# The down projection of a SwiGLU layer as one step of Strassen's scheme in four passes

## The chip, the core and the metric

The kernel runs on one core of a Trainium2 chip, in one launch. The core has five engines with an instruction stream each: TensorE (PE in the profile) multiplies matrices into PSUM, VectorE (DVE) and GpSimd (POOL) work elementwise, ScalarE (ACT) casts and evaluates functions, and SyncE (SP) issues the transfers between DRAM (HBM) and SBUF. The metric is the device time of one execution in microseconds (us), smaller is better. The median of three runs of the kernel before is 1910.74 us.

## What is computed

One layer of an encoder on 1152 rows (1024 frames of a prompt and 8 x 16 frames of running streams) of width 1024: three token mixers side by side, a cross-attention, and a SwiGLU feed-forward network, each with a residual add, and a final RMSNorm. The change touches the last matrix product of the feed-forward network, the residual add behind it, and the final norm.

```python
D_MODEL = 1024
...
D_FF = ((8 * D_MODEL + 3 * 256 - 1) // (3 * 256)) * 256   # 2816
EPS = 1e-6
...
def rmsnorm(x, g):
    xf = x.astype(jnp.float32)
    y = xf * lax.rsqrt(jnp.mean(xf * xf, axis=-1, keepdims=True) + EPS)
    return (y * g.astype(jnp.float32)).astype(x.dtype)
...
def swiglu(u, wg, wu, wd):
    hdn = jax.nn.silu(jnp.einsum('bnd,df->bnf', u, wg)) * jnp.einsum('bnd,df->bnf', u, wu)
    return jnp.einsum('bnf,fd->bnd', hdn, wd)
...
    h = h + swiglu(rmsnorm(h, p['norm_ffn_g']), p['w_gate'], p['w_up'], p['w_down']).astype(h.dtype)
...
    y_prompt = rmsnorm(hp, final_norm_g)
    y_sample = rmsnorm(hs, final_norm_g)
```

All of it is in float32.

## The kernel before

The kernel is one long program; each engine executes its instructions in the order in which a scheduler placed them, and waits for what they read. A tile from a pool with n buffers can be written again only when the readers of the tile n places earlier are done. Large products are taken in three matmuls on halves of the mantissa: each operand x is split into hi (a cast by ACT, L1697) and lo = x - hi (a subtraction by VectorE, L1701), and hi·hi + hi·lo + lo·hi is accumulated in PSUM (`mm3`, L328 to L330).

The last stages are these. Gate/up (`gate_up`, L1857 for its matmuls) makes the hidden rows of the feed-forward network, 22 tiles of 128 features by 1152 rows. It uses a scheme of seven products already: its right and left factors are sums of blocks (L1705, L1713, `sub`), split with POOL (L132) or VectorE, and its results are recombined from PSUM by VectorE (L1832). ACT and VectorE multiply the two branches (L1837, L1838), and SP stores each tile to the DRAM scratch `hid_sc` (L1839).

The down projection follows. It takes the rows in three chunks c of 384. For each of the 22 feature tiles f, SP loads a hidden tile of 128 x 384 (L1977, 192 KB) and a row block of w_down of 128 x 1024 (L1978, 512 KB); both are split; then three blocks of 128 rows times two column halves times three make 18 matmuls of 512 columns, accumulated over f in six of the eight PSUM banks:

```python
for i in range(3):
    for j in range(2):
        products(ops, i, j, f == 0, f == NFT - 1)
```

Behind each of the first two chunks `finish` adds the residual rows (loaded from `h_sc`), squares them on ACT, takes the power -1/2 on POOL with one Newton step on VectorE, scales (L1942) and stores. The last chunk holds back its last three f, and multiplies them block by block, so that `finish_by_halves` (L1952 to L1963) works on one block while PE multiplies the next. POOL has nothing but those small powers in this stage. All loads of the stage are issued by SP in order, and the stores of hidden and output rows stand in the same queue.

Of the kernel before, what the change touches and what calls it, by code (L numbers as in the profile page):

```python
# [17 lines left out]
P = 128  # L18
# [39 lines left out]
def f32(x):  # L58
    return x.bitcast(F32)
# [3 lines left out]
def tile_hybrid_step(ctx: ExitStack, tc: tile.TileContext, a: dict):  # L63
# [1599 lines left out]
    rawp = ctx.enter_context(f_pool("rawp", 2))  # L1663
    up = ctx.enter_context(f_pool("up", 3))
    tmp = ctx.enter_context(f_pool("tmp", 1))
    tlp = ctx.enter_context(f_pool("tlp", NL))
# [227 lines left out]
    trp = ctx.enter_context(f_pool("trp", NR, "right"))  # L1894
# [22 lines left out]
    bstack.close()  # L1917


    fin = ctx.enter_context(f_pool("fin", 1))  # L1920
# [5 lines left out]
    banks = [pd, pd, pS, pS, pT, pT, pT, lambda: o_all]  # L1926
    HALF = [slice(j * 512, (j + 1) * 512) for j in range(2)]

    def store_rows(b, j0, j1, y):
        cl = slice(j0 * 512, j1 * 512)  # L1930
        dst = a["y_prompt"][0, b * P:(b + 1) * P, cl] if b < 8 else a["y_sample"].rearrange("b q d -> (b q) d")[:, cl]
        SP.dma_start(out=dst, in_=y[:, cl])

    def finish(b, x, acc):

        for j in range(2):
            DVE.tensor_tensor(out=x[:, HALF[j]], in0=x[:, HALF[j]], in1=acc[j], op=ALU.add)
        y = fin.tile([P, D], F32, tag="y", name="y", bufs=4)
        ss = small(1)
        ACT.activation(y, x, AF.Square, accum_out=ss)  # L1940
        r = rstd_of(ss, 1, 1.0 / D)
        DVE.scalar_tensor_tensor(y, x, r, gF, ALU.mult, ALU.mult)  # L1942
        store_rows(b, 0, 2, y)

    def finish_by_halves(b, x):

        y = fin.tile([P, D], F32, tag="y", name="y", bufs=4)
        v, r, t, r2 = small(2), small(1), small(1), small(1)

        def half(j, acc):  # L1950
            ss = small(1)
            DVE.tensor_tensor(out=x[:, HALF[j]], in0=x[:, HALF[j]], in1=acc, op=ALU.add)  # L1952
            ACT.activation(y[:, HALF[j]], x[:, HALF[j]], AF.Square, accum_out=ss)
            if j == 0:
                DVE.tensor_scalar(v[:, 0:1], ss, 1.0 / D, EPS, ALU.mult, ALU.add)
                return
            DVE.scalar_tensor_tensor(v[:, 1:2], ss, 1.0 / D, v[:, 0:1], ALU.mult, ALU.add)
            POOL.tensor_tensor(out=r, in0=v[:, 1:2], in1=mhalf, op=ALU.pow)
# [76 lines left out]
```

## Time and profile before

| | |
|---|---|
| runs, device time | 1910.74 us median (1908.35 to 1920.12) |
| profiled execution, span from first to last instruction | 1911.2 us |
| mean granted clock of TensorE | 0.989 |
| first and last matmul of the down projection start | 1626.41 and 1902.21 us |

The page gives no time of the profiled execution outside its span. How to read the rows further on: the views list instructions, or groups of them, with their engine (PEld is the loading of TensorE's stationary operand), the line of the kernel, the operation, the tiles out<-in, partitions x elements and the count (x4). In a timeline the first number is the start and the second the duration in us, or for a group the time from the first start to the last end; in brackets stands the idle time ahead of it and what ended it. In the view by groups the busy time and the mean duration in ns of one stand behind the first bar, the idle time before and its releasers behind the second. In the view by stretches, busy time and count stand for each engine, then the granted clock, the busy share of the DMA engines and GB/s. The matmul rows' durations overlap, since matmuls are pipelined; the spacing of their starts is what one costs.

### The profile page before, as it was taken

To read this page: it belongs to the slowest core of one execution; us is meant where nothing else is said; L and a number is where in the kernel's file an instruction comes from. 1 tells how busy PE (TensorE), PEld (TensorE's weight loads), DVE (VectorE), ACT (ScalarE), POOL (GpSimd) and SP (SyncE) were. 2 spreads that over 40 slices of the span, in tenths; PEclk is the share of its full clock that TensorE was granted. 3 is DMA by queue.
4 is the path that set the end of the run, shared out by engine and by line. 5 is a ranking of instruction groups with operands and counts; after the bars stand their busy time and mean duration, and the time that the engine had idled before them with its cause. 6 is when DMAs were issued, how large, how long until landed. Compare 5 with 4: busy or idle time off the path is not lost.

```text
span 1911.2 us, 32463 instructions
## 1 busy us (share of the span) xinstructions
PE 1834.5 (96%) x12120; PEld 1637.6 (86%) x12120; DVE 894.3 (47%) x1823; ACT 822.7 (43%) x1779; POOL 627.9 (33%) x923
## 2 busy tenths in 40 slices
PE   7989988999998899999999999999999999999998
PEld 5889876888876677899998889999999999788886
DVE  3421323557656882354444487333333333455554
ACT  6531543535666870344343275333333333344443
POOL 7632416254224662211112105454444542000000
PEclk9999998999999999999999999999999999999999
DMA  9455645536579896345567124223322223566672
GB/s 338 141 165 159 207 139 129 161 102 186 174 237 291 268 323 217 111 144 162 180 210 270 61 83 119 70 71 81 88 73 70 70 70 104 188 196 228 183 245 91
DMA packets 302365, 306.07 MB, mean 160 GB/s; under 512 B 82428, under 2 KB 253668, under 8 KB 302208
## 3 DMA queue, kind: packets, MB, share of 16 engines
q1 hardware_dynamic: 302208, 304.01, 51.4%
q8 instruction: 95, 1.56, 0.3%
q14 instruction: 62, 0.51, 0.1%
HBM read 229.84 MB, written 74.63 MB: 159 GB/s over the span
## 4 chain that ended last, share of the span: by engine, by line
PE 81%; DMA 6%; DVE 3%; POOL 3%; issue 3%; ACT 2%; SPq 1%; POOLq 0%; DVEq 0%; ACTq 0%
PE psd L1857 11%; PE psd L328 10%; PE psd L329 10%; PE psd L330 9%; PE pst L1857 8%; PE pss L1857 4%; PE pss L328 3%; PE pss L329 3%; PE pss L330 3%; PE pso L1857 2%; PE pso L594 2%; PE pst L328 1%; PE pst L329 1%; PE pst L330 1%; POOL wl L132 1%
## 5 line engine op out<-in xcount | busy, mean ns | idle before, releaser
L132 POOL TENSOR_TENSOR wl<-wr,wh 128x256 fp32r<-128x256 f32 (+2 forms) x184 | 140.9, 800 | 219.4 <-ACT wh L292 215.7
L328 PE MATMUL psd<-act,wh 128*128 128x384 f32 x576 | 199.2, 346 | 4.8 <-DVE sg L455 2.7
L329 PE MATMUL psd<-act,wh 128*128 128x384 f32 x576 | 197.9, 344 | 0.0
L330 PE MATMUL psd<-act,wl 128*128 128x384 f32 x576 | 197.1, 342 | 0.0
L1857 PE MATMUL pst<-bT,tr 128*128 128x256 f32 (+1 forms) x1068 | 155.0, 293 | 0.0
L1857 PEld LDWEIGHTS pst<-bT,tr 128*128 128x128 f32 x1068 | 144.9, 188 | 0.1
L328 PE MATMUL psd<-wh,act 128*128 128x256 f32 (+3 forms) x414 | 133.7, 326 | 3.4 <-DMA act<-osc 1.5
L330 PE MATMUL psd<-wh,act 128*128 128x512 f32 (+3 forms) x424 | 136.6, 323 | 0.0
L329 PE MATMUL psd<-wl,act 128*128 128x256 f32 (+3 forms) x414 | 133.7, 324 | 0.0
L1857 PE MATMUL psd<-bT,tr 128*128 128x320 f32 (+1 forms) x912 | 132.9, 295 | 0.8 <-DVE tr L1701 0.5
L1857 PEld LDWEIGHTS psd<-bT,tr 128*128 128x128 f32 x912 | 124.7, 188 | 1.3 <-DVE tr L1701 0.7
L328 PEld LDWEIGHTS psd<-act,wh 128*128 128x128 f32 x576 | 109.3, 190 | 8.4 <-DVE sg L455 3.1
L132 POOL TENSOR_TENSOR tr<-u,tr 128x256 fp32r<-128x256 f32 x110 | 82.6, 780 | 100.2 <-ACT tr L1697 82.2
L329 PEld LDWEIGHTS psd<-act,wh 128*128 128x128 f32 x576 | 109.5, 190 | 1.5 <-issue 1.1
L330 PEld LDWEIGHTS psd<-act,wl 128*128 128x128 f32 x576 | 109.2, 190 | 1.3 <-issue 1.0
L132 POOL TENSOR_TENSOR ws<-ws 128x256 f32<-128x256 f32 (+2 forms) x100 | 70.1, 729 | 115.1 <-DVE ws L521 102.4
L253 POOL TENSOR_SCALAR sm<-sm 128x1 f32<-128x1 f32 (+2 forms) x27 | 8.3, 308 | 299.0 <-ACT y L1940 210.7
L1832 DVE TENSOR_TENSOR tr<-tr,pst 128x256 f32<-128x256 f32 (+1 forms) x86 | 38.6, 449 | 138.3 <-ACT tr L1829 105.1
L132 POOL TENSOR_TENSOR tr<-raw,tr 128x256 fp32r<-128x256 f32 x94 | 69.4, 767 | 85.6 <-ACT tr L1697 77.5
L1697 ACT CAST tr<-tr 128x384 fp32r<-128x384 f32 (+1 forms) x70 | 37.7, 538 | 121.4 <-DMA tr<-hidsc 119.0
L328 PEld LDWEIGHTS psd<-wh,act 128*128 128x128 f32 x414 | 79.2, 192 | 11.6 <-issue 1.8
L292 ACT CAST wh<-wr 128x512 fp32r<-128x512 f32 (+2 forms) x90 | 52.2, 621 | 80.9 <-PE psd L330 31.0
(622 smaller groups left out, 4697.9 us busy)
## 6 DMA issues: line engine op xcount, KB each, us to landing
u<-w_down SPq DMA_DIRECT2D x40, 512.0 KB
raw<-w_down SPq DMA_DIRECT2D x26, 512.0 KB
st<-qksc SPq DMA_DIRECT2D x48, 256.0 KB
wr<-w_in SPq DMA_DIRECT2D x44, 256.0 KB
tr<-hidsc SPq DMA_DIRECT2D x57, 192.0 KB
hidsc<-tr SPq DMA_DIRECT2D x34, 288.0 KB
qksc<-sg SPq DMA_DIRECT2D x48, 192.0 KB
wr<-cache_sb_k SPq DMA_DIRECT2D x32, 256.0 KB
```

The lines of the kernel that those rows point to most:

```text
L132: POOL.tensor_tensor(out=out[:, a0:a1], in0=in0[:, a0:a1], in1=in1[:, a0:a1], op=op)
L253: POOL.tensor_scalar(v, ss, inv, EPS, ALU.mult, ALU.add)
L292: ACT.copy(hi, raw)
L328: PE.matmul(out, ah, bh, start=start, stop=False)
L329: PE.matmul(out, ah, bl, start=False, stop=False)
L330: PE.matmul(out, al, bh, start=False, stop=stop)
L594: return PE.matmul(po[r:r + 64, q_], vt[:, 2 * (k0 + i) + j, :], pfs[i][:, sl], start=start and k0 == 0 and (j == 0 or qp > 0), stop=k0 + ...
L1697: ACT.copy(hi, src)
L1832: DVE.tensor_tensor(out=at(out, g), in0=at(x, g), in1=ps[g][:, :GW[g]], op=op)
L1857: PE.matmul(dst[g][:, :GW[g]], x[:, ka], y[:, k, :], start=start and k == 0 and m == 0, stop=stop and k == 3 and m == 2, skip_group_check= ...
```

## The change

The down projection of the 1024 prompt rows is taken by one step of Strassen's scheme (in Winograd's form) instead of plainly. A product of a 2 x 2 arrangement of blocks takes seven products of blocks instead of eight, on sums and differences of the blocks that are formed first, and with additions that recombine the results afterwards.

The work is arranged in four passes, over two groups g of four row blocks (512 rows) and two column parts s of 512 columns. A step of a pass takes two feature tiles (the two block rows of the 2 x 2), so a pass has 11 steps. Each step has a right side, from w_down (`down_right`: one load of 512 KB; differences on VectorE, L1950, and in part on POOL, L1952 and L1953; casts on ACT; the lo parts on VectorE, L1935), and a left side, from the hidden rows (`down_left`: one load of 512 KB, four sums of 256 columns on POOL, L1963, one cast and one subtraction of 1792 columns). The step's matmuls are seven products (the table PRODUCTS) for two row blocks, three each, all of 256 columns. All eight banks are used in each pass.

The first pass of a group also takes the 128 sample rows, plainly: the right side then keeps the hi and lo of all four plain blocks (splits of 1024 and 1024, otherwise of 768 and 1024), `down_sample` loads and splits 128 x 256 of hidden, and 12 more matmuls go into the half banks that the seven products leave free. The second pass of a group reuses the left sides of steps 5 to 10 of the first, mixed with new ones for steps 0 to 4. `combine` recombines a pass: additions from PSUM on VectorE, and additions to the rows on POOL. The sums of squares are taken by column part; `scale_rows` then scales and stores a block. The last pass holds back its last two steps, multiplies these for one row block of each pair after the other, and recombines, squares and scales behind each. The SBUF pools of gate/up are closed ahead of the stage and new ones opened. Nothing else is changed; the lines behind L1663 shift by one.

```diff
--- before.py
+++ after.py
+    gstack, trs = (ctx.enter_context(ExitStack()) for _ in range(2))
+    rawp = gstack.enter_context(f_pool("rawp", 2))
+    up = gstack.enter_context(f_pool("up", 3))
+    tmp = gstack.enter_context(f_pool("tmp", 1))
+    tlp = gstack.enter_context(f_pool("tlp", NL))
...
-    trp = ctx.enter_context(f_pool("trp", NR, "right"))
+    trp = trs.enter_context(f_pool("trp", NR, "right"))
...
+    gstack.close()
+    trs.close()
...
+    NST = NFT // 2
+    wrp, arp, spp, wfp, afp, fin = (ctx.enter_context(f_pool(n, b)) for n, b in (
+        ("wrp", 2), ("arp", 2), ("spp", 2), ("wfp", 2), ("afp", 6), ("fin", 1)))
...
+    def split_to(hi, lo, src):
+        ACT.copy(hi, src)
+        DVE.tensor_tensor(out=lo, in0=src, in1=f32(hi), op=ALU.subtract)
...
+    def down_right(j, s, whole):
+        t, at = blocks8(wrp, "dw")
+        SP.dma_start(out=t[:, 0:1024].rearrange("p (k c) -> p k c", k=2),
+                     in_=wd[2 * j * P:(2 * j + 2) * P, HALF[s]].rearrange("(k p) c -> p k c", p=P))
+        hi, lo = ([wfp.tile([P, 1024], F32R, tag=f"w{x}{i}", name=f"w{x}{i}") for i in range(2)] for x in "hl")
+        o = 0 if whole else 256
+        split_to(hi[0][:, o:], lo[0][:, o:], t[:, o:1024])
+        DVE.tensor_tensor(out=at(4, 2).rearrange("p (i c) -> p i c", i=2), in0=at(0).unsqueeze(1).to_broadcast([P, 2, 256]),
+                          in1=at(1, 2).rearrange("p (i c) -> p i c", i=2), op=ALU.subtract)
+        (POOL if whole else DVE).tensor_tensor(out=at(6), in0=at(2), in1=at(4), op=ALU.subtract)
+        POOL.tensor_tensor(out=at(7), in0=at(3), in1=at(6), op=ALU.subtract)
+        split_to(hi[1], lo[1], t[:, 1024:])
+        return [[x[i // 4][:, i % 4 * 256:i % 4 * 256 + 256] for i in range(8)] for x in (hi, lo)]
...
+    def down_left(j, g):
+        t, at = blocks8(arp, "da")
+        SP.dma_start(out=t[:, 0:1024].rearrange("p (k c) -> p k c", k=2),
+                     in_=hid_sc[2 * j:2 * j + 2, :, HALF[g]].rearrange("k p c -> p k c"))
+        for o, x, y, op in ((5, 0, 2, ALU.add), (4, 0, 1, ALU.subtract), (6, 5, 1, ALU.subtract), (7, 3, 6, ALU.subtract)):
+            POOL.tensor_tensor(out=at(o), in0=at(x), in1=at(y), op=op)
+        hi, lo = (afp.tile([P, 1792], F32R, tag=f"a{x}", name=f"a{x}") for x in "hl")
+        split_to(hi, lo, t[:, 256:])
...
+    def down_sample(j):
+        t = spp.tile([P, 256], F32, tag="sr", name="sr")
+        SP.dma_start(out=t.rearrange("p (k c) -> p k c", k=2),
+                     in_=hid_sc[2 * j:2 * j + 2, :, SEQ:T].rearrange("k p c -> p k c"))
...
+    PRODUCTS = ((1, 1, 2, 0), (3, 3, 0, 1), (7, 2, 0, 0), (2, 7, 1, 1), (5, 4, 1, 0), (6, 6, 2, 1), (4, 5, 3, 0))
...
+    def scale_rows(b):
+        v = var[b][:, 1:2]
+        r, t, r2 = small(1), small(1), small(1)
+        POOL.tensor_tensor(out=r, in0=v, in1=mhalf, op=ALU.pow)
+        DVE.scalar_tensor_tensor(t, r, -0.5, r, ALU.mult, ALU.mult)
+        DVE.tensor_tensor(out=t, in0=t, in1=v, op=ALU.mult)
+        DVE.scalar_tensor_tensor(r2, t, 1.5, r, ALU.add, ALU.mult)
+        for sl in HALF:
+            DVE.scalar_tensor_tensor(x[b][:, sl], x[b][:, sl], r2, gF[:, sl], ALU.mult, ALU.mult)
+            store_rows(b, sl.start, sl.stop, x[b])
...
+    def combine(g, s, p, acc):
+        x0, x1 = (x[4 * g + 2 * r + p][:, HALF[s]] for r in range(2))
+        w, u2, u3 = (fin.tile([P, n], F32, tag=t, name=t, bufs=2) for t, n in (("cw", 512), ("cu", 256), ("cv", 256)))
+        DVE.tensor_tensor(out=x1, in0=x1, in1=acc[0], op=ALU.add)
+        ACT.copy(w[:, 256:], acc[2][:, 0:256])
+        DVE.tensor_tensor(out=u2, in0=w[:, 256:], in1=acc[2][:, 256:], op=ALU.add)
+        DVE.tensor_tensor(out=w[:, 0:256], in0=u2, in1=acc[1][:, 0:256], op=ALU.add)
+        DVE.tensor_tensor(out=x0, in0=x0, in1=acc[1], op=ALU.add)
+        DVE.tensor_tensor(out=u3, in0=u2, in1=acc[3][:, 0:256], op=ALU.add)
+        pool_tt(x1, x1, w, ALU.add)
+        for h0 in (0, 256):
+            POOL.tensor_tensor(out=x0[:, h0:h0 + 256], in0=x0[:, h0:h0 + 256], in1=u3, op=ALU.add)
...
+    def down_pass(g, s, steps, left, sample, after, held):
+
+        acc = [[f() for f in fs] for fs in ((pS, pS, pd, pd), (pT, pT, pT, lambda: o_all))]
...
+        def mms(n, out, p, b, ah, al, bh, bl, last):
+            for m, (l, r) in enumerate(((ah, bh), (ah, bl), (al, bh))):
+                PE.matmul(out, l, r, start=m == 0 and (p, b) not in opened, stop=last and m == 2, skip_group_check=True)
+                opened.add((p, b))
...
+        def product(n, ops, i, p):
+            ia, ib, b, hf = PRODUCTS[i]
+            (ah, al), (bh, bl) = ops[:2]
+            sl = slice(p * P, (p + 1) * P)
...
+        for n, j in enumerate(steps):
+            if j not in left:
+                left[j] = down_left(j, g)
+            ops = (left[j], down_right(j, s, sample), down_sample(j) if sample else None)
...
+            if n >= NST - held:
+                keep.append((n, ops))
+                continue
+            for i in range(7):
+                for p in range(2):
+                    product(n, ops, i, p)
+                if i == 2 and sample:
+                    sample_rows(n, ops)
...
+        for p in range(2):
+            for i in (0, 5, 6, 4, 3, 1, 2):
+                for n, ops in keep:
+                    product(n, ops, i, p)
+            combine(g, s, p, acc[p])
+            if keep:
+                for r in range(2):
+                    squares(4 * g + 2 * r + p, s)
+                for r in range(2):
+                    scale_rows(4 * g + 2 * r + p)
...
+    straight = list(range(NST))
+    mixed_order = [5, 6, 0, 7, 1, 8, 2, 9, 3, 10, 4]
+    for g, (s0, s1) in enumerate(((0, 1), (1, 0))):
+        left = {}
+        down_pass(g, s0, straight, left, True, rows_of(g, 5), 0)
+        todo.extend([lambda b=4 * g + i: squares(b, s0) for i in range(4)] + [lambda: squares(8, g)])
+        if g == 1:
+            todo.append(lambda: scale_rows(8))
+        down_pass(g, s1, mixed_order, drop(left, range(5, NST)), False, rows_of(g, -1), 2 if g else 0)
+        if g == 0:
+            todo.extend([lambda b=i: (squares(b, 1), scale_rows(b)) for i in range(4)])
...
-        held, n_held = [], 3 if c == NCH - 1 else 0
-        for f in range(NFT):
-            raw, hid = raw2_t(), slot()[:, :CW]
-            SP.dma_start(out=hid, in_=hid_sc[f][:, c * CW:(c + 1) * CW])
-            SP.dma_start(out=raw, in_=wd[f * P:(f + 1) * P, :])
...
-            hh, hl = hi_lo(hid, CW, DVE)
-            ops = (hh, hl, [hi_lo(raw[:, j * 512:(j + 1) * 512], 512, DVE) for j in range(2)])
...
-            for i in range(3):
-                for j in range(2):
-                    products(ops, i, j, f == 0, f == NFT - 1)
```

The order of the instructions moves at three places. The first is VectorE, where gate/up ends. The L1838/L1839 rows multiply the two branches of hidden tiles (tl, tr); the L1832/L1833 rows add PSUM to the branches. Before:

```order
L1838 TENSOR_TENSOR tr<-tr,tl 128x576
L1832 TENSOR_TENSOR tl<-tl,pst 128x256
L1832 TENSOR_TENSOR tl<-tl,pst 128x320
L1838 TENSOR_TENSOR tl<-tl 128x576
L1701 TENSOR_TENSOR tl<-u,tl 128x512
L1701 TENSOR_TENSOR tr<-tl,tr 128x384
L1701 TENSOR_TENSOR tr<-raw,tr 128x512 x2
```

and after, with dw a raw right side, wh and wl its hi and lo, da, ah and al those of a left side, and sr, sh and sl those of the sample rows:

```order
L1839 TENSOR_TENSOR tr<-tr,tl 128x576
L1833 TENSOR_TENSOR tl<-tl,pst 128x256
L1935 TENSOR_TENSOR wl_17813<-dw,wh_17811 128x1024
L1833 TENSOR_TENSOR tl<-tl,pst 128x320
L1935 TENSOR_TENSOR wl_17814<-dw,wh_17812 128x1024
L1935 TENSOR_TENSOR wl_17896<-dw,wh_17894 128x1024
L1935 TENSOR_TENSOR wl_17897<-dw,wh_17895 128x1024
L1839 TENSOR_TENSOR tl<-tl 128x576
L1950 TENSOR_TENSOR dw<-dw 128x512 x2
L1935 TENSOR_TENSOR sl<-sr,sh 128x256 x2
L1935 TENSOR_TENSOR al<-da,ah 128x1792 x2
```

The last hidden product now stands behind the four splits of two right sides, and the first left side behind all of them.

The second place is POOL at the same point of the program. Before, its last splits for gate/up (raw, tr) are followed only by the small powers of the final norm (sm):

```order
L132 TENSOR_TENSOR tr<-raw,tr 128x256 x6
L132 TENSOR_TENSOR tr<-tr 128x256 x2
L132 TENSOR_TENSOR tr<-raw,tr 128x256 x6
L253 TENSOR_SCALAR sm<-sm 128x1
L254 TENSOR_TENSOR sm<-sm,mhalf 128x1
```

and after, a little into the first pass:

```order
L1952 TENSOR_TENSOR dw<-dw 128x256
L1953 TENSOR_TENSOR dw<-dw 128x256
L1963 TENSOR_TENSOR da<-da 128x256 x16
L1952 TENSOR_TENSOR dw<-dw 128x256
L1963 TENSOR_TENSOR da<-da 128x256 x2
L1953 TENSOR_TENSOR dw<-dw 128x256
L1963 TENSOR_TENSOR da<-da 128x256 x6
```

POOL's sums of left and right sides now run through the whole stage, in one queue.

The third place is POOL at the end of the program. Before, three powers for the last three blocks close it; after, all additions of the last pass stand ahead of all four powers (h the residual rows, cw and cv the recombined parts):

```order
L1953 TENSOR_TENSOR dw<-dw 128x256 x5
L132 TENSOR_TENSOR h<-h,cw 128x256 x2
L2020 TENSOR_TENSOR h<-h,cv 128x256 x2
L132 TENSOR_TENSOR h<-h,cw 128x256 x2
L2020 TENSOR_TENSOR h<-h,cv 128x256 x2
L2000 TENSOR_TENSOR sm<-var,mhalf 128x1 x4
```

The powers of the first two blocks thus come behind the recombination of the last two, and so does their scaling on VectorE.

More of the change, by code (lines that the diff above doesn't have):

```diff
@@ new lines, in down_left @@
+    def down_left(j, g):
[6 more added lines that the diff above has]
+        split_to(hi, lo, t[:, 256:])
+        return [[None] + [x[:, 256 * i:256 * i + 256] for i in range(7)] for x in (hi, lo)]
@@ L1931, in store_rows, with squares @@
         dst = a["y_prompt"][0, b * P:(b + 1) * P, cl] if b < 8 else a["y_sample"].rearrange("b q d -> (b q) d")[:, cl]
         SP.dma_start(out=dst, in_=y[:, cl])
-    def finish(b, x, acc):
-        for j in range(2):
-            DVE.tensor_tensor(out=x[:, HALF[j]], in0=x[:, HALF[j]], in1=acc[j], op=ALU.add)
-        y = fin.tile([P, D], F32, tag="y", name="y", bufs=4)
+    x, var = {}, {}
+    def squares(b, s):
         ss = small(1)
[L1940 to L1958, printed above, removed]
-            DVE.scalar_tensor_tensor(t, r, -0.5, r, ALU.mult, ALU.mult)
-            DVE.tensor_tensor(out=t, in0=t, in1=v[:, 1:2], op=ALU.mult)
-            DVE.scalar_tensor_tensor(r2, t, 1.5, r, ALU.add, ALU.mult)
-            for q in range(2):
-                DVE.scalar_tensor_tensor(y[:, HALF[q]], x[:, HALF[q]], r2, gF[:, HALF[q]], ALU.mult, ALU.mult)
-                store_rows(b, q, q + 1, y)
-        return half
@@ new lines, in squares @@
+        ACT.activation(fin.tile([P, 512], F32, tag="junk", name="junk", bufs=2), x[b][:, HALF[s]], AF.Square, accum_out=ss)
+        if b not in var:
+            var[b] = fin.tile([P, 2], F32, tag="var", name="var", bufs=9)
+            DVE.tensor_scalar(var[b][:, 0:1], ss, 1.0 / D, EPS, ALU.mult, ALU.add)
+        else:
+            DVE.scalar_tensor_tensor(var[b][:, 1:2], ss, 1.0 / D, var[b][:, 0:1], ALU.mult, ALU.add)
+    def scale_rows(b):
[8 more added lines that the diff above has]
+            store_rows(b, sl.start, sl.stop, x[b])
@@ new lines, in tile_hybrid_step, with rows_of, after @@
+    todo = []
+    def rows_of(g, n):
+        def after(k):
+            if k == n:
+                for b in [4 * g + i for i in range(4)] + [8] * (g == 0):
+                    x[b] = fin.tile([P, D], F32, tag="h", name="h", bufs=6)
+                    load_late(x[b], h_sc[b * P:(b + 1) * P, :])
+                if g == 0:
+                    load_late(gF, a["final_norm_g"].unsqueeze(0).to_broadcast([P, D]))
+            elif todo and k % 2 == 0:
+                todo.pop(0)()
+        return after
@@ new lines, in drop @@
+    def drop(left, steps):
+        return {j: left[j] for j in steps}
+    straight = list(range(NST))
[7 more added lines that the diff above has]
+        down_pass(g, s1, mixed_order, drop(left, range(5, NST)), False, rows_of(g, -1), 2 if g else 0)
+        if g == 0:
+            todo.extend([lambda b=i: (squares(b, 1), scale_rows(b)) for i in range(4)])
```

58 lines of the change are left out of this document (24 added, 34 removed).

## The prediction

> **What bounds the kernel now.** I read the page's busy table, then busy time by stretches, then the timeline of TensorE at both ends of the down projection, which is the only stage that changes.
>
> ```profile
> span 1911.2 us, 32463 instructions
> PE 1834.5 (96%) x12120; PEld 1637.6 (86%) x12120; DVE 894.3 (47%) x1823; ACT 822.7 (43%) x1779; POOL 627.9 (33%) x923
> core: us from the first to the last instruction, mean granted TensorE clock
> core 0: 1911.2 us, clock 0.989
> core 0: us, PE busy (x) PEld busy (x) DVE busy (x) ACT busy (x) POOL busy (x), PEclk, DMA share, GB/s
> 1186.00:1626.00 440.00, 440.00 (x3322) 440.00 (x3321) 161.10 (x282) 147.19 (x298) 199.21 (x269) 1.00 0.30 78
> 1640.00:1911.00 271.00, 260.41 (x1130) 212.68 (x1128) 138.88 (x246) 107.48 (x207) 8.28 (x15) 0.98 0.59 193
> ...
> 1623.23 3.34 PE L1857 MATMUL pst<-bT,tr 128*128 128x256 f32 x24
> 1626.41 0.40 PE L328 MATMUL psd<-tr 128*128 128x512 f32 x1
> 1626.64 0.39 PE L329 MATMUL psd<-tr 128*128 128x512 f32 x1
> ...
> 1902.21 0.40 PE L330 MATMUL psd<-tl,tr 128*128 128x512 f32 x1
> ```
>
> TensorE passes from gate/up (L1857) to down (L328 to L330) with no gap and runs to 1902.6: 276 us for 3 x 22 x 18 = 1188 matmuls of 512 columns, one each 0.23 us. The rest of the span, 8.6 us, is the tail. In that stage (second stretch) PE is busy 96% of the time, VectorE about half of it, and GpSimd (POOL) practically idle. So PE bounds it, and work removed from PE counts only as far as the other engines keep up. The profiled span is 0.5 us from the median of the runs, 1910.74; the page gives no time outside it, so I forecast against both as one.
>
> **What the change takes from PE.** It issues 4 passes x 11 steps x 42 = 1848 matmuls, and 2 x 11 x 12 = 264 for the sample rows: 2112, all of 256 columns. Between the next two rows start twelve of that shape.
>
> ```profile
> 1445.20 0.40 PE L1857 MATMUL pst<-bT,tr 128*128 128x256 f32 x2
> ...
> 1446.61 0.46 PE L1857 MATMUL pst<-bT,tr 128*128 128x320 f32 x2
> ```
>
> That is 1.41 / 12 = 0.1177 us, so 2112 x 0.1177 = 248.6 us, 27.4 us less than before. One step is 54 x 0.1177 = 6.36 us of PE with sample rows, 42 x 0.1177 = 4.94 without.
>
> **What it adds to VectorE and GpSimd.** Per step it forms sums and differences ahead of the splits. Per right side with sample rows, VectorE subtracts 512 columns and splits 2 x 1024, and POOL does two of 256; without them VectorE also does one of POOL's and splits 1024 and 768. Per left side (32 of them: 11, 5, 11, 5) POOL does four of 256, and VectorE splits 1792. Per sample step VectorE splits 256 more. Counted: VectorE 208 subtractions with 175,616 columns, and POOL 22 + 44 + 128 = 194 operations of 256. Each alone would fit under 248.6 us: before, VectorE takes 0.69 for 512, POOL 0.74.
>
> ```profile
> L1701 DVE TENSOR_TENSOR tr<-u,tr 128x512 fp32r<-128x512 f32 x59 | 39.2, 689 | 2.6 <-PE pss L329 0.7 <-ACT tr L1697 0.5 <-PE pst L329 0.4
> L1701 DVE TENSOR_TENSOR tr<-tr 128x384 fp32r<-128x384 f32 x48 | 26.8, 558 | 94.1 <-ACT tr L1697 94.1
> L132 POOL TENSOR_TENSOR tr<-tr 128x256 fp32r<-128x256 f32 x26 | 18.6, 737 | 0.0
> L1697 ACT CAST tr<-u 128x512 fp32r<-128x512 f32 x63 | 36.6, 616 | 2.6 <-PE pst L329 1.0 <-PE pss L330 1.0 <-PE psd L330 0.4
> L1697 ACT CAST tr<-tr 128x384 fp32r<-128x384 f32 x51 | 26.2, 513 | 118.1 <-DMA tr<-hidsc 115.7 <-PE pss L330 2.4
> ```
>
> But they don't run beside each other. In gate/up there is a place where both queue:
>
> ```profile
> 1495.51 3.74 POOL L132 TENSOR_TENSOR tr<-u,tr 128x256 fp32r<-128x256 f32 x4 [5.34 <-ACT tr L1697]
> ...
> 1496.22 1.27 DVE L1713 TENSOR_TENSOR tl<-u 128x512 f32<-128x512 f32 x1 [1.17 <-PE psd L1857]
> 1497.52 1.12 DVE L1705 TENSOR_TENSOR u<-u 128x512 f32<-128x512 f32 x1
> 1498.56 0.41 DVE L1832 TENSOR_TENSOR tr<-tr,pss 128x256 f32<-128x256 f32 x1
> 1498.89 0.90 DVE L1705 TENSOR_TENSOR u<-tl,u 128x512 f32<-128x512 f32 x1
> 1499.93 0.69 DVE L1705 TENSOR_TENSOR u<-u 128x512 f32<-128x512 f32 x1
> ```
>
> Subtractions of 512 end at 1497.49 and 1498.64, 1.15 apart: one POOL operation stood between. POOL's four end at 1499.25 and the waiting one ends at 1499.79, 0.54 later; alone (last row) it takes 0.69. The addition from PSUM (L1832) isn't held up. So a subtraction with both inputs in SBUF and a POOL operation take turns, VectorE's turn of 512 being 0.55 and POOL's 1.15 - 0.55 = 0.60. Columns cost 512 / 0.55, nearly 1 ns each (the rows of 512 and 384: 131 ns for 128); I take N / 0.96 ns + 0.014 us, which gives 0.547 for 512, and as an estimate 1.08 for 1024, 1.88 for 1792, 0.28 for 256.
>
> In turns: VectorE's 208 are 175,616 / 960 + 208 x 0.014 = 186 us; 194 of POOL are 116 us; the recombination puts 32 more on POOL (19 us); the final scaling is 18 of 512 (10 us). Sum 331 us, against 248.6 on PE. A sample step is 4.87 + 6 x 0.60 = 8.5 us of turns where PE has 6.36; a step with a new left but no sample 7.6 against 4.94; one that reuses a left 3.3. So PE stops being the bound.
>
> The Trainium skill ("SBUF — State Buffer", section "SBUF: two separate sides") says that whichever of the two starts first holds the shared port pair for its whole instruction, and the other fully blocks. That speaks against the change still more: with whole instructions (an estimate from the same rows: VectorE 227 us, POOL 226 x 0.74 = 167) the turns would sum to 394 us and the time to about 2060. The rows agree that they block each other, but a pair took 1.15, not 0.69 + 0.74 = 1.43; so I keep the measured turn.
>
> **The start.** PE's first operand moves too. The order shows three splits of 1024 ahead of the last hidden product, about 3.2 us. SP's queue holds the first left load (da) behind the store of that product.
>
> ```profile
> 1627.85 0.76 DVE L1838 TENSOR_TENSOR tl<-tl 128x576 f32<-128x576 f32 x1 [0.75 <-ACT tl L1837]
> 1628.64 3.21 DMA hidsc<-tl
> 1631.87 3.64 DMA tl<-hidsc
> ...
> 1640.33 7.77 DMA tr<-hidsc
> ...
> 1646.67 0.39 PE L330 MATMUL pst<-tr 128*128 128x512 f32 x1
> 1649.27 0.50 PE L328 MATMUL psd<-tr 128*128 128x512 f32 x1 [2.20 <-ACT tr L1697]
> 1650.07 0.54 PE L328 MATMUL psd<-tr 128*128 128x512 f32 x1
> 1650.41 0.63 PE L328 MATMUL pss<-tr 128*128 128x512 f32 x1
> ...
> 1653.40 0.47 PE L330 MATMUL pst<-tr 128*128 128x512 f32 x1
> ```
>
> Today that store starts at 1628.6, three f steps are loaded before it, and PE doesn't notice until 1646.7. After: store about 1632, da issued just behind, landed 3.6 to 4 us on, 1636; four POOL operations 2.9; ACT's cast of 1792 about 1.66 (from 0.513 and 0.617 for 384 and 512); VectorE's split 1.9, beside the first products. PE starts at about 1641, and after such an idle time has half the clock for about 3.4 us (the rows from 1650.07 stand 0.43 apart instead of 0.23, after 2.2 us idle): +1.7. Step 0 ends near 1649.5 where 1626.6 + 6.4 = 1633.0 was possible: 16.5 us lost, between 10 (splits not in the way, turns short) and 20 (a landing with several transfers queued took 7.77). The sum below takes from this only the 1636.2 at which da lands and the turns can run; the 16.5 stand in the rival in which PE bounds.
>
> **The tail.** Before, the last matmul is followed by 8.6 us, all of it one block's work.
>
> ```profile
> 1905.22 0.16 DVE L1957 SCALAR_TENSOR_TENSOR sm<-sm 128x1 f32<-128x1 f32 x1
> 1906.05 0.16 DVE L1959 SCALAR_TENSOR_TENSOR sm<-sm 128x1 f32<-128x1 f32 x1 [0.66 <-POOL sm L1958]
> 1906.24 0.16 DVE L1960 TENSOR_TENSOR sm<-sm 128x1 f32<-128x1 f32 x1
> 1906.43 0.16 DVE L1961 SCALAR_TENSOR_TENSOR sm<-sm 128x1 f32<-128x1 f32 x1
> 1906.63 1.41 DVE L1963 SCALAR_TENSOR_TENSOR y<-h,sm,gF 128x512 f32<-128x512 f32 x2
> 1907.41 1.00 SPq L1932 DMA_DIRECT2D y_sample<-y  x2
> ```
>
> After, POOL's order has the four powers behind all recombination additions, and VectorE scales four blocks behind them: recombination 2.7 us and 2 POOL operations to 4.4, squares and sums 1.0, power and its wait 0.8, four blocks of about 0.5 + 1.4, less what runs beside it, store and landing about 3.2 (from 1908.0 in the last row to the end at 1911.2): some 16.4 us. Bounds 8.6 (three blocks done under the matmuls) and 20 (all serial).
>
> **The sum.** Turns count from 1636.2, when da lands: about 8 us of them are done by then (four splits, two subtractions, four on POOL), and 7 belong to the tail, so 331 - 8 - 7 = 316 remain: 1952.5. PE still has two held steps, 84 x 0.1177 = 9.9: 1962.4. Waits inside a step: the da and dw buffers are two deep, and a buffer's round (landing 3.4, POOL's four turns with VectorE's between them 4 to 7, cast 1.7, split 1.9) is 11 to 14 us for two steps of 8.5, so mostly covered. Bounds 0 and one uncovered landing in each of the 22 sample steps, 75 us; nearer to 0, a quarter: 19. PE ends at 1981, and with the tail 1998. The pass boundaries cost nothing beyond this while turns bound (PE waits anyway); SP moves less than before (44 + 32 blocks of 512 KB against 66 of 512 and 66 of 192), and ACT's four casts of a sample step, 4096 columns at the rows' 0.81 ns and 0.2 us each, are 4.1 us.
>
> **Rivals.**
> - Turns hidden: VectorE and POOL seldom queue together, or their waits stay below PE's time. For it: each alone fits. Against: six POOL operations in every sample step and the rows of 1496. Then 1626.6 + 16.5 + 248.6 + 3.4 (three boundaries of about 1.1: a copy of 256 by ACT, an addition from PSUM of 0.41, and their waits) + 16.4 = 1911.5, no change.
> - The saving comes through: start and tail as today too, 1626.6 + 248.6 + 8.6 = 1884, faster. It decides only if the turns per step fall under PE's 6.36 and the first da lands by 1628. Both contradict rows above.
> - Buffers: rounds of da and dw don't fit two steps, each sample step also waits for a landing: 1998 - 19 + 75 = 2054. For it: dw passes VectorE and POOL in alternation. Against: SP has no other work.
>
> **How the numbers follow.** Turns bound: 0.82, 1998. Turns hidden: 0.07. Saving through: 0.02. Buffers: 0.09. The range is that of the first case: low with no waits and today's tail, 1962.4 + 8.6 = 1971, less 5% of the turns (16) for a turn of 1024 or more that I only extrapolate, 1955; high with 10 us at start and tail together and half of the 75, 1998 + 10 + 37 = 2045. About 1% is what a measurement of this kernel can tell from no change, so faster 0.02, same 0.07, slower 0.91.
>
> **What would show it.** In the down stage PE's share falls to about 70%, with gaps that end on VectorE's al or wl, or ACT behind them. POOL's mean for 256 rises from 0.74 to above 1, VectorE's for 512 towards 1.1. The first product starts near 1641. The passes end near 1740, 1828, 1912 and 1981. I am wrong if VectorE and POOL show durations like those when alone, or if PE's gaps end on a DMA.

## The result, and the profile after

The changed kernel takes 2003.66 us (median of 4 runs, 2000.14 to 2009.23) against 1912.59 us for the kernel before in the same session (1908.35 to 1920.12): a ratio of 1.048, with a 95% interval of 1.0448 to 1.0512. It is slower by 91 us. The forecast was 1998, with a range of 1955 to 2045.

The page of the changed kernel, its span, the busy time of the engines, and four rows of the busy tenths in 40 slices (a slice is 50 us):

```profile
span 2005.0 us, 34480 instructions
PE 1853.7 (92%) x13044; PEld 1695.6 (85%) x13044; DVE 1054.4 (53%) x1877; ACT 866.4 (43%) x1743; POOL 898.3 (45%) x1143
...
PE   7989989999998899999999999999999968787886
...
DVE  3421333557567843534444863333343347898986
...
POOL 7532524525135543111021064444444428989863
PEclk9999999999999999999999999999999989988898
```

In the last seven slices, the down projection, VectorE and POOL are both mostly at 8 or 9 where POOL stood at 0 before, and TensorE falls from 9 to 7 or 8. The same by stretches, with gate/up first and the down projection second:

```profile
1186.00:1626.00 440.00, 440.00 (x3320) 440.00 (x3319) 158.23 (x276) 146.54 (x296) 205.19 (x277) 1.00 0.28 71
1640.00:2005.00 365.00, 291.13 (x2112) 281.24 (x2112) 298.38 (x307) 155.03 (x182) 273.77 (x227) 0.89 0.42 138
```

Gate/up is as it was. In the second row VectorE (third value after the length) is busy for 298 us and POOL for 274 of 365; together 572 us, so in at least 207 us both count as busy. In most of such time one of them is waiting for the other, as the durations in the groups of that stretch show (mean ns of one behind the comma):

```profile
L1935 DVE TENSOR_TENSOR wl<-dw,wh 128x1024 fp32r<-128x1024 f32 x62 | 92.3, 1495 | 17.4 <-ACT wh L1934 17.2
L1935 DVE TENSOR_TENSOR al<-da,ah 128x1792 fp32r<-128x1792 f32 x32 | 72.5, 2267 | 18.9 <-ACT ah L1934 18.9
L1950 DVE TENSOR_TENSOR dw<-dw 128x512 f32<-128x512 f32 x40 | 38.3, 958 | 16.1 <-DMA dw<-w_down 16.1
...
L2012 DVE TENSOR_TENSOR h<-h,pss 128x512 f32<-128x512 f32 x4 | 2.7, 677 | 0.0
...
L1963 POOL TENSOR_TENSOR da<-da 128x256 f32<-128x256 f32 x128 | 160.5, 1272 | 28.7 <-DMA da<-hidsc 22.2 <-DVE dw L1952 2.1 <-DVE wl L1935 2.0
```

POOL's sums of 256 last 1.27 us on the mean where such an operation took 0.74 alone; VectorE's differences of 512 last 0.96 instead of 0.69. The addition of 512 from PSUM (L2012) takes 0.68 as ever. A place in the first pass, VectorE first and POOL behind it:

```profile
1719.05 2.55 DVE L1935 TENSOR_TENSOR al<-da,ah 128x1792 fp32r<-128x1792 f32 x1
1721.53 0.95 DVE L1935 TENSOR_TENSOR sl<-sr,sh 128x256 fp32r<-128x256 f32 x1
1722.40 3.44 DVE L1935 TENSOR_TENSOR wl<-dw,wh 128x1024 fp32r<-128x1024 f32 x2
...
1719.68 2.51 POOL L1952 TENSOR_TENSOR dw<-dw 128x256 f32<-128x256 f32 x1
1722.16 2.60 POOL L1963 TENSOR_TENSOR da<-da 128x256 f32<-128x256 f32 x2
```

The split of 1792 ends at 1721.60; POOL's operation, which has stood since 1719.68, ends at 1722.19, 0.59 later; the split of 256 ends at 1722.48, 0.29 after that. I have taken such distances between successive ends from the whole stage of the trace, for instructions that were already standing when the other engine's ended (VectorE's with both inputs in SBUF alone):

```
turn (us), 1636 to 1990        count   median    forecast
POOL 256                         146    0.595     0.60
VectorE 256                       22    0.283     0.28
VectorE 512                       35    0.548     0.547
VectorE 768                       14    0.816     0.81
VectorE 1024                      42    1.082     1.08
VectorE 1792                      20    1.882     1.88
neither at such an operation    22.1 us in all
```

The size of a turn, read before at one place with 512 columns, holds up to 1792, and four in five of POOL's 146 lie between 0.584 and 0.603. In the whole stage there are only 22 us in which no turn is being taken. So waits for loads, buffers or anything else that leaves both engines without work can have cost no more than these 22 us between 1636 and 1990.

The beginning and the end of TensorE's work in the stage:

```profile
1626.40 3.34 PE L1858 MATMUL pst<-bT,tr 128*128 128x256 f32 x24
1641.65 0.58 PE L2029 MATMUL pso<-wh,sh 128*128 128x256 f32 x1 [11.91 <-ACT sh L1934]
...
1647.13 0.58 PE L2029 MATMUL psd<-wh,ah 128*128 128x256 f32 x1 [3.78 <-ACT ah L1934]
...
1988.65 0.28 PE L2029 MATMUL pst<-wh,al 128*128 128x256 f32 x1
```

TensorE waits 12 us for the first sample rows and 4 more for the first left side. The four passes' last matmuls start at 1737.7, 1821.7, 1918.1 and 1988.7. From the start of the last one to the end of the span are 16.4 us, from its end 16.1.

### The profile page after: what moved, and what is told of

The parts are those of the page before. It is cut to its first block, busy times and chain, and to the rows that moved or that the text cites. A ratio compares the mean times of both kernels' runs of the same rounds, so it can differ in the third digit from the quotient of the medians.

```text
span 2005.0 us, 34480 instructions
## 1 busy us (share of the span) xinstructions
PE 1853.7 (92%) x13044; PEld 1695.6 (85%) x13044; DVE 1054.4 (53%) x1877; ACT 866.4 (43%) x1743; POOL 898.3 (45%) x1143
## 3 DMA queue, kind: packets, MB, share of 16 engines
q8 instruction: 103, 1.69, 0.3%
## 4 chain that ended last, share of the span: by engine, by line
PE 67%; DVE 10%; POOL 8%; DMA 7%; issue 4%; ACT 4%; SPq 0%; DVEq 0%; POOLq 0%; ACTq 0%
PE psd L1858 10%; PE psd L328 8%; PE psd L329 8%; PE pst L1858 8%; PE psd L330 8%; PE pss L1858 4%; POOL da L1963 2%; DVE wl L1935 2%; PE pss L328 2%; PE pss L329 2%; POOL wl L132 2%; PE pss L330 2%; PE pso L1858 2%; DVE al L1935 2%; DMA dw<-w_down 1%
## 5 line engine op out<-in xcount | busy, mean ns | idle before, releaser
L1963 POOL TENSOR_TENSOR da<-da 128x256 f32<-128x256 f32 x128 | 160.5, 1272 | 28.7 <-DMA da<-hidsc 22.2
L1934 ACT CAST wh<-dw 128x1024 fp32r<-128x1024 f32 (+1 forms) x88 | 86.2, 993 | 118.7 <-POOL dw L1953 56.6
L1935 DVE TENSOR_TENSOR wl<-dw,wh 128x1024 fp32r<-128x1024 f32 (+1 forms) x88 | 124.9, 1430 | 17.7 <-ACT wh L1934 17.5
L1833 DVE TENSOR_TENSOR tr<-tr,pst 128x256 f32<-128x256 f32 (+1 forms) x86 | 38.6, 449 | 139.2 <-ACT tr L1830 106.0
```

The source lines that it names most:

```text
L1833: DVE.tensor_tensor(out=at(out, g), in0=at(x, g), in1=ps[g][:, :GW[g]], op=op)
L1934: ACT.copy(hi, src)
L1935: DVE.tensor_tensor(out=lo, in0=src, in1=f32(hi), op=ALU.subtract)
L1963: POOL.tensor_tensor(out=at(o), in0=at(x), in1=at(y), op=op)
```

## The experiments

The theory: a subtraction of VectorE with both inputs in SBUF and an operation of POOL exclude each other, and the sum of their turns, not TensorE, sets the time of the stage. The rivals: the engines are independent and the time is the latency of load, sum, cast and split in buffers two deep; the transfers bound; or the late first product is what costs. Of the kernels with a profile the text also gives the stage's own time, from the start of the last gate/up matmul to the end of the span, since the end of gate/up moves by some us between executions (last section): 285.0 us in the kernel before, 375.6 in the changed one.

**Additions on POOL in the kernel before.** If turns exist, they must show without any Strassen step. Six additions by POOL per f step, 396 in all, whose result nobody reads:

```diff
+            for i in range(6):
+                POOL.tensor_tensor(out=extra, in0=raw[:, 0:256], in1=raw[:, 512:768], op=ALU.add)
             hh, hl = hi_lo(hid, CW, DVE)
```

> The kernel before with six additions of 256 columns on POOL for each of the 66 f steps of the down projection, from the loaded block of w_down into a tile that nobody reads: nothing waits for them but the buffer of w_down. Turns: a step of f has 3 subtractions on VectorE (2 x 0.55 + 0.41 = 1.51 us) and 6 x 0.60 on POOL, 5.1 us against 4.1 us of TensorE, so up to 66 x 1.0: 1960 to 1985 us. Independent engines (rival): POOL alone needs 6 x 0.70 = 4.2 us, VectorE 1.9, neither much above 4.1: 1911 to 1922 us.

Measured: 2008.98 us in a single run, against a median of 1913.5 for the kernel before on that chip; the stage has 379.1 us. The groups of the stage, VectorE's splits and some of POOL's additions, and the longest wait of SP:

```profile
L1701 DVE TENSOR_TENSOR tr<-u,tr 128x512 fp32r<-128x512 f32 x59 | 63.5, 1108 | 40.0 <-ACT tr L1697 40.0
L1701 DVE TENSOR_TENSOR tr<-tr 128x384 fp32r<-128x384 f32 x48 | 47.0, 980 | 24.7 <-ACT tr L1697 24.7
...
L1987 POOL TENSOR_TENSOR ex<-u 128x256 f32<-128x256 f32 x222 | 197.4, 889 | 17.0
...
SPq L1979 <- POOL ex L1987: 240.1, 55, 5.8
```

Idle engine time was filled with work whose result nobody reads, and the kernel became 95 us slower. Splits of 512 went from 0.69 to 1.11 us. The direction is the theory's; the size is above its 1960 to 1985, for two reasons that the trace shows. Only about half of POOL's operations follow one of VectorE's and cost 0.60; those behind another of POOL's cost about 0.81. And the additions of the held steps stand in POOL's queue ahead of the powers of the final norm, so from the start of the last matmul to the end there are 22.3 us instead of 9.0.

The rival was priced too low as well. The additions do hold something, the buffer of w_down: SP waited 240 us for them before its next loads (last row). At 0.81 us each, POOL alone needs 396 x 0.81 = 321 us where TensorE needs 276, so by this estimate independent engines would lose some 45 us here, and with the 13 us at the end 58 of the 95. They don't explain the rest, nor the longer splits. Distances between successive ends, added up as turns, make 344 us (POOL 238, VectorE 107) of the 357 between the last gate/up matmul and the last of the stage. With two additions instead of six the sum of turns stays below TensorE's time:

> The kernel before with two POOL additions of 256 columns per f step instead of the six of the run before. Turns: 1.51 + 2 x 0.60 = 2.7 us per f step, below TensorE's 4.1 us: no change, 1905 to 1920 us, though VectorE's mean for 512 rises from 0.69 to about 0.9 us. A rival, in which POOL beside VectorE costs time in proportion to its operations (a third of the 95 us of six): about 1945 us.

Measured: 1916.93 us (10 runs) against 1913.58 (13 runs), a ratio of 1.002 (1.0006 to 1.0034). So 132 additions cost 3 us and 396 cost 95: a cost in proportion is out. Between turns and independent engines this run doesn't decide, since POOL alone would need only 132 x 0.81 = 107 us.

```profile
L1701 DVE TENSOR_TENSOR tr<-u,tr 128x512 fp32r<-128x512 f32 x59 | 40.7, 720 | 0.9 <-ACT tr L1697 0.4 <-PE pst L329 0.3
L1701 DVE TENSOR_TENSOR tr<-tr 128x384 fp32r<-128x384 f32 x48 | 33.6, 700 | 87.8 <-ACT tr L1697 83.9 <-PE psd L330 2.8 <-PE pss L329 1.1
```

The mean for 512 rose to 0.72 only, not to 0.9: POOL's two additions mostly fall on the splits of 384 (0.56 before, 0.70 now).

**POOL's sums moved to VectorE.**

```diff
-        (POOL if whole else DVE).tensor_tensor(out=at(6), in0=at(2), in1=at(4), op=ALU.subtract)
-        POOL.tensor_tensor(out=at(7), in0=at(3), in1=at(6), op=ALU.subtract)
+        DVE.tensor_tensor(out=at(6), in0=at(2), in1=at(4), op=ALU.subtract)
+        DVE.tensor_tensor(out=at(7), in0=at(3), in1=at(6), op=ALU.subtract)
...
-            POOL.tensor_tensor(out=at(o), in0=at(x), in1=at(y), op=op)
+            DVE.tensor_tensor(out=at(o), in0=at(x), in1=at(y), op=op)
```

> The changed kernel with all sums of the left and right sides (194 operations of 256 columns) on VectorE; POOL keeps the recombination and the powers. Turns (theory): an operation of 256 takes POOL a turn of 0.60 us, VectorE 0.28 to 0.34, so the queue of turns loses some 62 us; it gets back up to 22 (VectorE's operations back to back cost 0.06 us each more than after a turn of POOL) and some 15 (the additions from PSUM stood beside POOL's turns and now stand in line). Net about -25: 1960 to 1990 us, means of VectorE as when alone (512 near 0.70, 1024 near 1.23). Independent engines (rival: the time is the latency of load, sum, cast, split in two-deep buffers): VectorE's busy time rises by 65 us and it is late more often, so no gain, 2003 us or more. Transfers bound (rival): 2003 us.

Measured: 1984.55 us (4 runs, 1982.37 to 1985.74), a ratio of 1.036 (1.0324 to 1.0395) to the kernel before: 19 us less than the changed kernel, though 194 operations left the less loaded engine for the more loaded one.

```profile
L1935 DVE TENSOR_TENSOR wl<-dw,wh 128x1024 fp32r<-128x1024 f32 x62 | 75.2, 1217 | 3.9 <-ACT wh L1934 3.6
...
L1963 DVE TENSOR_TENSOR da<-da 128x256 f32<-128x256 f32 x128 | 50.2, 422 | 8.0 <-DMA da<-hidsc 7.9
...
1640.00:1981.00 341.00, 280.36 (x2112) 270.66 (x2112) 299.27 (x493) 154.93 (x182) 43.35 (x41) 0.92 0.45 148
```

VectorE's means are those of an engine alone, and its busy time in the stage is 299 us, as much as in the changed kernel with its waits (298). By the expectation independent engines would have lost by this, and turns gain. One thing besides turns is better in this kernel: a sum of 256 takes VectorE 0.42 us and POOL 0.74, so the way from a load to its cast is shorter too.

**Either side of the queue taken away.** First POOL's sums:

```diff
-        for o, x, y, op in ((5, 0, 2, ALU.add), (4, 0, 1, ALU.subtract), (6, 5, 1, ALU.subtract), (7, 3, 6, ALU.subtract)):
-            POOL.tensor_tensor(out=at(o), in0=at(x), in1=at(y), op=op)
...
+        src = t[:, 0:896].unsqueeze(1).to_broadcast([P, 2, 896])
```

> The changed kernel without POOL's 194 sums: the 22 + 44 of the right sides and the 128 of the left sides are left out (casts and splits of the same number of columns read other columns of the loaded tiles), so the prompt rows of the output are not the reference's. VectorE, ACT, SP and TensorE do what they did. Turns: VectorE alone has 4.9 us in a sample step and 3 to 5.5 in another, below TensorE's 6.36 and 4.94, so TensorE bounds: gate/up's end, 17 us at the start, 248.6, boundaries 3, waits about 8, tail 16 make 1915 to 1930 us. Transfers or buffers bound (rival): the landings and buffer depths are unchanged, so most of the loss stays: above 1960 us.

Measured: 1932.1 us in a single run, stage 300.1: 2 us above the range that turns gave, far below the rivals' 1960.

```profile
1640.00:1930.00 290.00, 261.28 (x2112) 258.32 (x2112) 234.44 (x307) 153.93 (x182) 40.36 (x41) 0.96 0.53 174
```

Then VectorE's splits, first by filling lo with zeros:

```diff
-        DVE.tensor_tensor(out=lo, in0=src, in1=f32(hi), op=ALU.subtract)
+        DVE.memset(f32(lo), 0.0)
```

> The changed kernel with the lo parts of the down projection set to zero by VectorE (142 fills of the same number of columns that read nothing from SBUF) instead of subtracted: the lo parts are left out of the product. POOL keeps its 194 sums, VectorE its 66 differences of 512 and 256. Turns: what is left is 116 to 135 us for POOL and 30 for VectorE, far below TensorE's 248.6, if a fill needs no turn: 1915 to 1930 us, POOL's mean for 256 near 0.75 us. Transfers or buffers bound (rival): above 1960 us. If a fill needs a turn as well, near 2000 us, and the run says nothing.

Measured: 1959.73 us in a single run, stage 334.7, between what either side expected. Taken alone it told nothing, because the edit brought waits of its own (the last two rows are those of the whole stage: us in total, times, longest):

```profile
1634.47 1.55 DVE L1935 MEMSET al<- 128x1792 f32 x1 [0.32 <-issue]
1636.34 1.55 DVE L1935 MEMSET al<- 128x1792 f32 x1 [0.32 <-issue]
...
1638.36 0.75 DVE L1839 TENSOR_TENSOR tl<-tl 128x576 f32<-128x576 f32 x1
...
DVE dw L1950 <- DMA dw<-w_down: 59.9, 21, 10.2
...
DVE wl L1935 <- PE psd L2029: 14.9, 1, 14.9
```

A fill waits for no data, so six of them (the last two are shown) were placed ahead of the last hidden product (L1839), whose store stands ahead of the first da; TensorE's first product came 22.4 us after gate/up, 10 later than in the changed kernel. In the passes the fills of the right sides wait some 28 us for TensorE to release their tiles, 14.9 of it at once (last row), with VectorE's differences for POOL behind them in the queue; and these differences wait 60 us for loads of dw, which is what the buffers rival names. How these waits make up the rest of the loss stays open. The next kernel has the same loads and buffers of dw and da, and no fills in the passes: all lo parts are one tile.

```diff
+    zero = fin.tile([P, 1792], F32R, tag="zero", name="zero")
+    DVE.memset(f32(zero), 0.0)
...
         ACT.copy(hi, src)
-        DVE.tensor_tensor(out=lo, in0=src, in1=f32(hi), op=ALU.subtract)
...
-        hi, lo = (afp.tile([P, 1792], F32R, tag=f"a{x}", name=f"a{x}") for x in "hl")
+        hi, lo = afp.tile([P, 1792], F32R, tag="ah", name="ah"), zero
```

> The changed kernel in which all lo parts of the down projection are one tile of zeros, filled once: the 142 subtractions of VectorE are left out, and the lo parts of the product with them; TensorE, ACT, SP and POOL do what they did. Turns: POOL's 194 sums alone (0.70 each back to back, 136 us) and VectorE's 66 differences (30 us) are far below TensorE's 248.6: a gap of 12 to 14 us at the start as in the run without POOL's sums, and 1915 to 1935 us in all, POOL's mean near 0.75 us. Rival (latency of load, sum, cast in two-deep buffers, which is what it was up to the cast): above 1960 us.

Measured: 1917.96 us in a single run, stage 284.0, and 1914.62 when it was timed again with the kernel before (10 runs; ratio 1.0001, 0.9988 to 1.0015):

> The run with one tile of zeros in place of all lo parts, timed: 1912 to 1922 us, beside the same with the early start.

```profile
1640.00:1915.00 275.00, 256.38 (x2112) 255.88 (x2112) 97.14 (x169) 153.59 (x182) 175.13 (x228) 0.97 0.55 183
...
L1964 POOL TENSOR_TENSOR da<-da 128x256 f32<-128x256 f32 x128 | 102.1, 819 | 30.9 <-DMA da<-hidsc 23.7 <-ACT wh L1936 4.0 <-ACT ah L1936 0.6
```

The rows are those of the single run. POOL does the same 194 sums behind the same loads, and TensorE has no gap above 0.3 us from the second pass on. With either partner gone, and no fills in its place, the loss of 91 us shrinks to between 1 and 19. It is not VectorE's work that is too much, and not POOL's, but their sum. One limit: whoever takes out the sums or the splits also shortens the time for which a buffer of da or dw is held, so by themselves these two runs don't tell turns from buffers; a kernel with three buffers was not run. Against buffers as the main cost stand the 22 us of the changed kernel in which neither engine has a turn.

**The start.** The first da and the first dw get the memory that gate/up frees first, the second ones that which it frees last.

```diff
-        ("wrp", 2), ("arp", 2), ("spp", 2), ("wfp", 2), ("afp", 6), ("fin", 1)))
+        ("wr0", 1), ("ar0", 1), ("spp", 2), ("wr1", 1), ("ar1", 1), ("wfp", 2), ("afp", 6), ("fin", 1)))
```

> The changed kernel with the raw tiles of left and right sides in four pools of one buffer (dw, da, then sr, then dw, da) instead of two of two, the same memory in another order: the first da and the first dw then lie where gate/up frees its memory early, and step 0's loads, sums and splits are done before gate/up ends, while the second dw waits. Turns: about as many turns are taken by 1640 us as in the changed kernel (two splits of a right side less, a left side more), so no change although TensorE starts some 10 us earlier: 1997 to 2009 us. Rival (the time of TensorE's first product is what costs): 6 to 16 us less than 2003.7, 1988 to 1997 us.

Measured: 2004.2 us (4 runs, 2002.02 to 2010.95) against the changed kernel's 2003.66. No change, although TensorE now starts at once:

```profile
1627.22 0.90 PE L1858 MATMUL pst<-bT,tr 128*128 128x320 f32 x5
1627.96 0.27 PE L2031 MATMUL pso<-wh,sh 128*128 128x256 f32 x1
...
1644.25 0.58 PE L2031 MATMUL psd<-wh,sh 128*128 128x256 f32 x1 [9.10 <-ACT wh L1935]
```

Of the 12 us, 9 came back as the gap ahead of step 1 (last row), the first pass ends 103.9 us after gate/up instead of 108.3, and by the end most of the rest is gone too: the last matmul starts 358.1 us after gate/up's last, 359.2 in the changed kernel, so 1.1 us of the 12 are left. In the kernel with the tile of zeros, TensorE binds, and there the same edit should count:

> The run with one tile of zeros in place of all lo parts (142 subtractions and the lo parts of the product left out), with the pools of the run in which step 0 is made before gate/up ends. Turns no longer bound, TensorE does, so now the earlier start must count: the 10 us gap at the end of gate/up goes, one gap of about 9 us with its half clock stays ahead of step 1 (its da and dw are loaded behind the last hidden store): 5 to 9 us less than the run with zeros alone. Rival (an early start is worth nothing here, as in the changed kernel): no difference to it.

Measured: 1912.86 us (10 runs, 1905.98 to 1919.32) beside 1914.62: 1.8 us less, with ratios to the kernel before of 0.9994 (0.9978 to 1.0011) and 1.0001 (0.9988 to 1.0015) that overlap. In the profiles the stage takes 280.6 us instead of 284.6. The sign fits, the size is below the 5 to 9, and the runs can't tell it from nothing. What the gain met is seen in the trace: the gap of 10 us is gone, one of 5.3 us stands ahead of step 1, whose dw is now loaded last, one of 1.3 us ahead of the first product with the zero tile, and the first pass is 81.1 us long instead of 78.2; the second is 3 us longer too. So the pair of runs doesn't show that an early start counts more where TensorE binds.

**Half the change.** If the sum of turns is the price, fewer Strassen steps, beside plain ones that leave VectorE idle, should hide it. Rows 512 to 1023 plainly first, rows 0 to 511 and the sample rows by two passes:

```diff
+    plain_pass()
     left = {}
-    for g, (s0, s1) in enumerate(((0, 1), (1, 0))):
...
+    down_pass(0, 0, straight, left, True, rows_of(0, 5), 0)
...
+    down_pass(0, 1, mixed_order, drop(left, range(5, NST)), True, rows_of(0, -1), 2)
```

> Strassen's step for four of the eight prompt blocks only: rows 512 to 1023 plainly first (11 steps of 48 matmuls of 512, in eight banks), then two passes over rows 0 to 511 with the sample rows in both; sums on VectorE, and the first da and dw in early memory as in the run before. TensorE: 528 x 0.2283 + 1188 x 0.1177 = 120.5 + 139.8 = 260.3 us against 276 before and 248.6 in the changed kernel. Turns of a Strassen step 7.2 us for TensorE's 6.36, less the left sides that are made during the plain part (VectorE has 3.4 us of work there per 11 us): hidden. 1627 + 260.3 + 3 (start) + 3 (boundaries) + 0 to 6 + 16 (tail) = 1909 to 1916 us: no change against the kernel before. Rival (a loss per Strassen pass that has nothing to do with turns, about 10 us as between TensorE's share and the passes of the run with sums on VectorE): 1925 to 1940 us.

Measured: 1929.06 us (4 runs, 1924.75 to 1930.29), a ratio of 1.0074 (1.005 to 1.0099): 0.7% slower than the kernel before, and slower than forecast. TensorE should have had 260.3 us and its work stretched over 284: the plain part 127.1 us for 120.5 (one gap of 4.6 us, where the second da stands behind two dw in SP's queue), the first Strassen pass 81.9 for 69.9, the second 74.4 for 69.9; then 15.6 from the start of the last matmul. A stretch of 80 us that is nearly all of the first pass (1755 to 1837):

```profile
1750.00:1830.00 80.00, 72.55 (x558) 70.20 (x557) 73.13 (x129) 38.67 (x51) 10.78 (x4) 0.98 0.57 187
```

VectorE is busy for 73.1 of these 80 us. It carries work that the forecast had left out, finishing the four plain blocks: three of their eight additions of 0.68 fall in this pass and five shortly before, and all eight scalings of 0.7, on a VectorE that by forecast already had 7.2 us per step for TensorE's 6.36. The rival (10 us a pass) named about the right time, but not evenly: 12 and 4.5.

None of these kernels is faster than the kernel before by more than the measurement can tell. The most that the scheme could bring here is 27 us of TensorE (1.4%), and start, tail and VectorE's work cost as much or more even where half of it is done.

## Why the prediction was right

**TensorE's work.** Forecast 2112 x 0.1177 = 248.6 us. Where nothing else bound it (the tile of zeros, passes two and four), 462 matmuls took 55.3 us, 0.120 each: 253 us for all. Right to 2%.

**Turns.** The step that carried the forecast, 331 us of turns instead of 248.6 of TensorE, was read from six rows at one place of gate/up, and is confirmed by the sizes in the table and by the runs: both sides of the queue removed in turn, moved, and imitated in the kernel before. The largest doubt, whether a turn of 1024 or 1792 goes by the same rule, is answered: 1.082 and 1.882 us. The sum itself was some 4% low. Added up from the trace as distances between successive ends, all turns take 345 us (VectorE 204, POOL 141), because not every operation follows one of the other engine: a third of POOL's follow another of its own or an idle time, and take 0.70 or 0.73 instead of 0.60.

The Trainium skill ("SBUF — State Buffer", section "SBUF: two separate sides") has the port pair held for the whole instruction, with the other engine fully blocked. The trace agrees that the two block each other, in both directions; that a port pair is the reason no run here shows. With whole durations, by the estimate in the prediction, the rule would have given some 2060 us. Measured are 2003.66, and a turn of POOL of 0.595 us where the whole instruction alone takes 0.74; so about 0.15 us of POOL's instruction seems to run beside the other engine's.

**Waits.** Forecast 19 us, a quarter of an upper bound and the weakest number of the sum; in the trace no turn is taken in 22.1 us, which counts every wait and not only the uncovered landings that the 19 stood for. This was luck as much as reasoning.

**The start.** Forecast: da landed at 1636.2, first product of a left side at 1641. POOL began on da at 1640.4, that product came at 1647.1, in an execution in which gate/up ended 3.2 us later. That TensorE's first product started at 1641.65, as the forecast "near 1641" has it, is luck: it was one of the sample rows, which the forecast of the start had left out. Less the shift the landing was right to 1.0 us and the first product of a left side 3 us late: POOL's four sums took until 1645.3, with sums for the next left side among them, and ACT's cast of 1.69 came after them. It didn't matter: in the run with an early first step, of 12 us gained at the start 1.1 were left at the end of the stage.

**The passes** were forecast to end near 1740, 1828, 1912 and 1981 and did at 1737.7, 1821.7, 1918.1 and 1988.7. The third was 12 us longer than forecast (96.4 for 84): it carries the recombination of the second, and the squares and scalings of the first four blocks, which the sum had but the division into passes had not. Errors of both signs made the sum better than its parts: the turns were 14 us more than forecast, and the two held steps, which stood in the sum with 9.9 us of TensorE behind the last turn, cost less, since only 32 of their matmuls (3.8 us) come after the last split.

**The tail**: 16.4 forecast, 16.1 measured from the end of the last matmul, from which the forecast counts.

**The signs.** TensorE's waits in the stage end on ACT's casts (48 us) and on VectorE's wl and al (16 us), with 4 us on recombination and none on a load, as forecast. ACT's casts in turn waited 47 us for loads of dw, so loads do stand in the chain; but VectorE and POOL had other turns to take meanwhile. TensorE's share fell to 80% and not to 70%: the mean granted clock was 0.89 (0.98 before), and 271 of its 2112 matmuls stand about 0.22 us apart instead of 0.12, so they count as busy for longer. VectorE's mean for 512 rose to 0.96, where the forecast said towards 1.1.

**Small slips.** 1636.2 and 316 make 1952.2 and not 1952.5; a start at 1641 with 6.4 and 1.7 us ends step 0 at 1649.1 and not 1649.5. Neither moves the forecast by more than 0.4 us.

**The rivals.** Hidden turns would have given 1911.5, and removing either partner gave 1914.6 to 1932, so the price fits its condition. Buffers (2054) asked for a landing waited for in each sample step; the 22 us without a turn refute that size, and the tile of zeros agrees (same loads, same depth, no loss), though its buffers are held for a shorter time. The saving coming through (1884) was reached by no kernel.

## What to carry to other kernels

Two engines that are each half idle are not two free engines: before work is moved to POOL or VectorE, look in the trace for a place where both queue on SBUF operands, take the distance between successive ends as the turn of each, and add the turns to one sum as if they were one engine. A scheme that saves matmuls by sums pays in exactly this sum; here 27 us of TensorE stood against 331 - 249 us. And when two engines are named as one queue, ask the trace how long neither of them is at work: 22 of 354 us left no room for another cause of that size. An early first product was a weaker test here: it brought nothing where turns bound, and nothing that could be told from noise where TensorE did.

## What was not expected

The end of gate/up, whose instructions are the same in all these kernels but for a few rows, moves by several us between profiled executions (each of another kernel, and not all on one chip): its last matmul starts at 1623.0, 1625.9, 1626.3, 1629.4, 1631.8 and 1636.2 in six of them. A difference of a few us between two spans says little, and the stage's own time says more.

A fill by VectorE takes no turn: the 26 of 1792 columns in the passes lasted 1.55 us each, as long as those ahead of the stage, though POOL was at work beside 14 of them from start to end. And POOL's own operations stand 0.695 us apart behind each other but end 0.595 us behind one of VectorE's, so two engines that take turns lose less than their durations alone would suggest; here it was not enough to win.
